# Low parts of the down chunks by VectorE instead of an adding DMA, and other rates for the conditioning products

## The chip, the cores and the metric

One Trainium2 chip, and one of its cores. The metric is the device time of one execution of the whole program in microseconds (us). Engines are named as in the profile: PE is TensorE's matmul, PEld its weight load, DVE is VectorE, ACT is ScalarE, POOL is GpSimd, SP is SyncE, which here only issues DMAs. Each engine runs its own list of instructions strictly in order; a name with a q (SPq, POOLq) is an engine's sequencer.

## What is computed

Two transformer blocks in float32 on 256 tokens of width 1024. The first block (attention of three kinds, a gated merge, an FFN with a short convolution) comes first and is not touched. The second block has two layers on a latent stream and a context stream, each conditioned by products of a vector with a weight `w_mod`:

```python
m_lat = adaln_mod(c, w_mod[l], b_mod[l])          # 9 x 1024 numbers a layer, for each stream
m_ctx = adaln_mod(c_ctx, w_mod[l], b_mod[l])[None]
x_lat = ffn_sublayer(x_lat, m_lat, 0, norm_g[l, 0], ffn_w_in[l, 0], ffn_w_out[l, 0])
x_ctx = ffn_sublayer(x_ctx, m_ctx, 0, norm_g[l, 0], ffn_w_in[l, 0], ffn_w_out[l, 0])
...   # the mixer: attention, Fourier branch, gates; then the second FFN of the layer

def swiglu(u, w_in, w_out):
    a, b = jnp.split(u @ w_in, 2, axis=-1)
    return (jax.nn.silu(a) * b) @ w_out

def ffn_sublayer(x, m, i, g, w_in, w_out):
    u = modulate(rms_norm(x, g), m, i)
    return x + 0.5 * m[:, 3 * i + 2][:, None] * swiglu(u, w_in, w_out)
```

In layer 1 the context stream ends after the mixer's keys and values, so the last FFN runs on the latent stream alone. An FFN has a hidden width of 2816, which is 22 pieces of 128.

## The kernel before

**Products in three.** Every float32 weight chunk of 128 partitions is split into a high part `wh`, rounded to the matmul's input type, and a low part `wl = wr - wh`; each product is three matmuls (lines 500 to 502): high by high, low by high, high by low. A chunk comes through three rings: `wr` (the raw weights, 3 buffers, loaded from SP's queue, line 434), `wh` and `wl` (5 buffers each). `prefetch` makes the split ahead of the matmuls, and `load_to` asks for the raw chunk three further on; that DMA waits in SP's queue until the raw buffer of three chunks before is free, and everything behind it on SP waits too.

**Two ways to the low part.** `split_high` makes `wh` on ACT (line 439). For weights whose name is in `ADDED` it also writes `-wh` into `wl` on ACT (line 444), and a DMA issued by POOL adds the raw chunk to it (line 445); the raw buffer is free when that DMA has landed. For all others `split_low` makes one subtraction on DVE (line 453), and the raw buffer is free after it:

```python
if self.order[i][0].tensor.name[3:].startswith(ADDED):       # split_high
    self.nc.scalar.activation(lo[:, :n], r[:, :n], AF.Copy, scale=-1.0)
    self.nc.gpsimd.dma_start(lo[:, :n], r[:, :n], accum_op=ALU.add)
self.nc.vector.tensor_tensor(lo[:, :n], r[:, :n], h[:, :n].bitcast(F32), op=ALU.subtract)   # split_low
```

**The FFNs of the second block.** In order: FFN (0,0); mixer 0; FFN (0,1); FFN (1,0); mixer 1; FFN (1,1). The two in the middle, (0,1) and (1,0), are the "seven" FFNs: most of their up products are taken in pairs of chunks with seven products in the place of eight (`ffn7`, matmuls on line 1451). The pairs' weights are prepared by `pair_prep` with sums on DVE (lines 362, 372, 381, 405). Their downs come in four groups of 5, 5, 6 and 6 hidden pieces; a group has 8 chunks (one for 128 outputs each) of 640 or 768 columns. The first two chunks of a group run together in both "mm" banks of PSUM, then one chunk after the other; each ends in two additions into `x` on DVE (line 1184), which free the bank for the chunk after the next. After three of the groups comes a stretch of pairs, and the first 6 hidden pieces of a seven FFN are made in the ordinary way.

**Conditioning products.** `w_mod` is 288 units of 128x512. A unit is one DMA into one of three `wm` buffers (line 633, on SP's queue between the weight loads) and one or two products with a row sum on DVE (line 647; two for both streams, one where only the latent stream is wanted): 512 products in all. They are spread as filler: after a chunk with a tick, `run` adds a rate to a credit and runs a unit for every whole one. The rates are constants: `MR[2]` for FFN (0,0), `MR[3]` and `MR[4]` for the heads of mixer 0 and 1, `MG` for the end of a mixer (from its Fourier part on: chunks `w_ao`, `w_fo`, `w_o`), `MD` for the downs of the seven FFNs and the projections that follow. `mod_cols` runs what is still missing when a column is needed.

Of the kernel before, what the change touches and what calls it, by code (L numbers as in the profile page):

```python
# [35 lines left out]
SCRATCH = 1024  # L36
NRAW = 3
NMOD = 3
MR = (1.2, 0.5, 1.9, 0.0, 0.0)
MG = 2.0  # L40
MD = 1.3
ADDED = ("ffn_up01", "ffn_up10", "ffn_down01", "ffn_down10")
AT0 = (2.25, 0.5, 3.25, 5.5, 8, 2.25, 4, 2.67, 0.1)
AT1 = (2, 0.5, 3, 5, 9, 2, 4.5, 4, 0.1)
GL1 = (0, 1, 1, 1, 1, 1, 1, 1)
# [205 lines left out]
class Net:  # L251
# [185 lines left out]
    def split_high(self, i, n):  # L437
        h = self.wp.tile([P, D], F32R, name="wh")
        self.nc.scalar.activation(h[:, :n], self.raws[i][:, :n], AF.Copy)  # L439
        self.wts[i] = (h,)  # L440
        if self.order[i][0].tensor.name[3:].startswith(ADDED):

# [241 lines left out]
    def b1_attention(self):  # L684
# [288 lines left out]
        ev += [(4, lambda: nx["n"].ssq(self.sxx))] + [(ME[0] + ME[1] * d, norm_u, d) for d in range(KD)]  # L973
        ev += [(ME[2], mem_load), (ME[2] + 1, table2, 1), (22, self.setup_late), (31, mods_on, MR[0]), (60, mods_on, MR[1]), (AB[3] + 1, table3, 1)]
        ev += [(ME[3] + ME[4] * d, me, "sqadd", d) for d in range(KD)] + [(ME[5], me, "ssq"), (ME[6], mem_rb)]
# [118 lines left out]
    def b1_ffn(self):  # L1094
# [60 lines left out]
        def u(d):  # L1155
            n["y"].u(d, self.c00[:, 1, 1], self.c00[:, 0, 1])
# [7 lines left out]
        def rest():  # L1164
            self.cur = self.c00
            self.mod_rate = MR[2]
            self.pending = [(0.5 * d, lambda d=d: u(d)) for d in range(PC[0], KD, 2)]
# [219 lines left out]
    def ffn7(self, wu, groups, gh, gl, up, down):  # L1387
# [67 lines left out]
        def front(f, i):  # L1455
            self.pair_prep(i, 2)
            s = st[f] = {"w": self.prep[i], "c": self.bank("ps")[:, CTX], "e": self.bank("ps")[:, CTX]}
            product(1, s["w"], "ab", 0, s["c"], True)
            nc.scalar.activation(s["e"], s["c"], AF.Copy)
# [130 lines left out]
        for g, (f0, f1) in enumerate(groups):  # L1590
# [6 lines left out]
            if g:  # L1597
                self.do(drain, prev[-1], prev[-2])
            self.do(self.set_rate, MD)
            down(g)  # L1600
            if f < NF:
                self.steps.insert(len(self.steps) - 1, ((), lambda f=f: front(f, self.pairs[0]), (), False))
        self.do(self.set_rate, MD)

# [32 lines left out]
    def mixer(self, l, both, nxt):  # L1637
# [53 lines left out]
        self.do(heads)  # L1691
        self.do(self.set_rate, MR[3 + l])
        bg = []
# [17 lines left out]
        def gates(d, at="mm"):  # L1711
            return [x for j in range(2) for x in self.chunk(w[28 + j * KD + d], cs, gate_done(d, j), at,
                                                           pieces=4 if both else 2)]
# [133 lines left out]
        for t in range(2):  # L1847
            self.do(f_split, nt // 2 - 1, t)
        self.do(f_const)
        self.do(self.set_rate, MG)  # L1850
        rest = [x for d in range(ng, 2 if both else KD) for x in gates(d, "ps")]
        if not both:
            self.steps += rest[:OO]
# [264 lines left out]
```

## Time and profile before

| | us |
|---|---|
| median of three runs | 2565.48 (2562.25 to 2566.53) |
| the profiled execution | 2564.71 |
| its span | 2562.9 |
| PE busy | 2468.2 (96%) |
| DVE busy | 1811.1 (71%) |
| ACT busy | 1230.7 (48%) |
| POOL busy | 136.0 (5%) |

The stages of the second block in the profiled execution: FFN (0,0) from 503 to 853 us, mixer 0 to 1278, FFN (0,1) to 1672, FFN (1,0) to 2056, mixer 1 to 2346, the last FFN to the end. A row of the order of time has its start, its duration, engine, line, operation and tiles; brackets at its end give how long the engine had stood idle and what released it. Matmuls overlap, so the time from one start to the next is shorter than the duration of one.

### The profile page before, as it was taken

The numbers are of one execution on the slowest core, as the hardware profiler recorded it, in microseconds if no ns is written. First come the engines' busy times: TensorE is split into PE (matmuls) and PEld (weight loads), VectorE is DVE, ScalarE is ACT, GpSimd is POOL, SyncE is SP. The second block draws the span as 40 slices with busy tenths as digits, with TensorE's granted clock in tenths as the row PEclk, the third lists the DMA queues.
The fourth block names the chain that finished last, engine by engine and source line by source line (L and its number), as shares of the span: only waits on it lengthen the run. The fifth ranks groups of instructions, "written<-read, shape, count | busy, mean of one in ns | idle before, by whom it ended". The sixth has DMA issues, their size and how long they took to land. (4 is left out here: it accounts for less than half of the span.)

```text
span 2562.9 us, 41264 instructions
## 1 busy us (share of the span) xinstructions
PE 2468.2 (96%) x15912; PEld 2214.6 (86%) x15912; DVE 1811.1 (71%) x3659; ACT 1230.7 (48%) x2175; POOL 136.0 (5%) x152
## 2 busy tenths in 40 slices
PE   8999999999999999999999899999999999998998
PEld 6899899998888878888887898888898878888998
DVE  6878787767878768688747577546577557777765
ACT  6755566542222356532354454554454545654543
POOL 0000200200000000100011100111100100000000
PEclk9999999999999999999999999999999999999999
DMA  7666456555655421155666536576536533355654
GB/s 252 211 216 224 138 183 195 160 165 170 204 189 182 136 75 58 56 168 185 193 154 177 137 103 189 146 168 178 128 118 185 145 120 105 112 178 190 190 186 132
DMA packets 144918, 410.16 MB, mean 160 GB/s; under 512 B 16273, under 2 KB 23121, under 8 KB 144337
## 3 DMA queue, kind: packets, MB, share of 16 engines
q1 hardware_dynamic: 132048, 371.87, 44.7%
q0 software_dynamic: 12672, 35.66, 8.0%
q8 instruction: 125, 2.05, 0.3%
q14 instruction: 73, 0.59, 0.1%
HBM read 370.73 MB, written 4.23 MB: 146 GB/s over the span
## 5 line engine op out<-in xcount | busy, mean ns | idle before, releaser
L439 ACT ACTIVATE wh<-wr 128x1024 fp32r<-128x1024 f32 (+2 forms) x503 | 506.5, 1009 | 425.1 <-DMA wr<-in_ffn_down 82.8
L453 DVE TENSOR_TENSOR wl<-wr,wh 128x1024 fp32r<-128x1024 f32 (+1 forms) x415 | 497.0, 1203 | 42.3 <-ACT wh L439 42.0
L501 PE MATMUL ps<-uh,wl 128*128 128x256 f32 (+2 forms) x1432 | 453.4, 317 | 4.6 <-DMA wl<-wr 2.7
L502 PE MATMUL ps<-ul,wh 128*128 128x256 f32 (+2 forms) x1432 | 453.4, 317 | 3.3 <-DVE ul L151 1.9
L500 PE MATMUL ps<-uh,wh 128*128 128x256 f32 (+2 forms) x1432 | 454.3, 317 | 0.1
L647 DVE SCALAR_TENSOR_TENSOR mjunk<-wm,cvec 128x512 bf16<-128x512 f32 x512 | 327.4, 686 | 67.0 <-DMA wm<-in_w_mod 66.6
L500 PE MATMUL mm<-gh,wh 128*128 128x512 f32 (+1 forms) x860 | 299.4, 348 | 32.6 <-DVE x L1184 26.3
L501 PE MATMUL mm<-gh,wl 128*128 128x512 f32 (+1 forms) x860 | 297.6, 346 | 0.8 <-DMA wl<-wr 0.8
L502 PE MATMUL mm<-gl,wh 128*128 128x512 f32 (+1 forms) x860 | 297.2, 346 | 0.0
L501 PEld LDWEIGHTS ps<-uh,wl 128*128 128x128 f32 x1432 | 273.6, 191 | 24.0 <-DMA wl<-wr 3.4
L502 PEld LDWEIGHTS ps<-ul,wh 128*128 128x128 f32 x1432 | 273.2, 191 | 22.1 <-DVE ul L148 2.3
L500 PEld LDWEIGHTS ps<-uh,wh 128*128 128x128 f32 x1432 | 273.1, 191 | 18.1 <-ACT uh L144 0.3
L500 PE MATMUL mm<-uh,wh 128*128 128x256 f32 (+1 forms) x840 | 281.7, 335 | 0.8 <-ACT uh L142 0.7
L502 PE MATMUL mm<-ul,wh 128*128 128x256 f32 (+1 forms) x840 | 271.6, 323 | 0.5 <-DVE ul L153 0.5
L501 PE MATMUL mm<-uh,wl 128*128 128x256 f32 (+1 forms) x840 | 271.1, 323 | 0.0
L500 PEld LDWEIGHTS mm<-gh,wh 128*128 128x128 f32 x860 | 165.3, 192 | 59.1 <-issue 15.0
L502 PEld LDWEIGHTS mm<-gl,wh 128*128 128x128 f32 x860 | 165.2, 192 | 20.5
L501 PEld LDWEIGHTS mm<-gh,wl 128*128 128x128 f32 x860 | 165.3, 192 | 20.3 <-DMA wl<-wr 1.2
L500 PEld LDWEIGHTS mm<-uh,wh 128*128 128x128 f32 x840 | 158.8, 189 | 25.1 <-issue 9.2
L502 PEld LDWEIGHTS mm<-ul,wh 128*128 128x128 f32 x840 | 158.5, 189 | 14.3 <-DVE ul L153 0.9
L501 PEld LDWEIGHTS mm<-uh,wl 128*128 128x128 f32 x840 | 158.9, 189 | 11.6
L1184 DVE SCALAR_TENSOR_TENSOR x<-mm,mc,x 128x256 f32<-128x256 f32 x212 | 93.4, 478 | 84.5 <-PE mm L502 84.4
(431 smaller groups left out, 5011.3 us busy)
## 6 DMA issues: line engine op xcount, KB each, us to landing
wr<-in_ffn_up SPq DMA_DIRECT2D x186, 512.0 KB, 4.2
wm<-in_w_mod SPq DMA_DIRECT2D x288, 256.0 KB, 4.0
wr<-in_w_in SPq DMA_DIRECT2D x106, 512.0 KB, 3.7
wr<-in_w_ffn_up SPq DMA_DIRECT2D x44, 512.0 KB, 4.2
wr<-in_ffn_down SPq DMA_DIRECT2D x48, 384.0 KB, 3.4
wr<-in_ffn_down SPq DMA_DIRECT2D x32, 512.0 KB, 3.7
wr<-in_w_v SPq DMA_DIRECT2D x24, 512.0 KB, 3.6
wl<-wr POOLq DMA_DIRECT2D x24, 512.0 KB, 5.9
```

Of the source, the lines that this page charges most:

```text
L439: self.nc.scalar.activation(h[:, :n], self.raws[i][:, :n], AF.Copy)
L453: self.nc.vector.tensor_tensor(lo[:, :n], r[:, :n], h[:, :n].bitcast(F32), op=ALU.subtract)
L500: mm(ps, lhsT=h, rhs=xh[k][:, cs], start=start and i == 0, stop=False)
L501: mm(ps, lhsT=lo, rhs=xh[k][:, cs], start=False, stop=False)
L502: mm(ps, lhsT=h, rhs=xl[k][:, cs], start=False, stop=stop and i == len(kk) - 1)
L647: nc.vector.scalar_tensor_tensor(junk, w, 1.0, self.cvec[:, v, cs], op0=ALU.mult, op1=ALU.mult, accum_out=self.m[l][:, v, h, j:j + 1])
L1184: self.nc.vector.scalar_tensor_tensor(x, ps[:, off:off + S], c[:, 2, v, d:d + 1], x, op0=ALU.mult, op1=ALU.add)
```

## The change

```diff
-MR = (1.2, 0.5, 1.9, 0.0, 0.0)
-MG = 2.0
-MD = 1.3
-ADDED = ("ffn_up01", "ffn_up10", "ffn_down01", "ffn_down10")
+MR = (1.2, 0.5, 2.3, 0.0, 0.4)
+MG = (2.3, 0.8)
+MD = 1.0
+ADDED = ("ffn_up01", "ffn_up10")
...
-        self.do(self.set_rate, MG)
+        self.do(self.set_rate, MG[l])
```

Two things change. The 64 down chunks of the seven FFNs get their low part from DVE (line 453); the 64 copies on ACT (line 444) and the 64 adding DMAs on POOL (line 445) go. And the 512 conditioning products stand elsewhere. Counted in the lists of instructions, before and after: 70 and 70 ahead of FFN (0,0), 194 and 234 in it, 138 and 152 in mixer 0, 48 and 19 in FFN (0,1), 24 and 19 in FFN (1,0), 38 and 18 in mixer 1. Of the 18 left in mixer 1, 6 stand in its value projections and 12 among its heads; before, 7 stood there, none among the heads, and 31 in its end. No matmul is added, removed or moved.

DVE's list in the second group of downs of FFN (0,1), before (`x<-mm,mc,x` are the additions that free a bank, `mjunk` the conditioning products):

```order
L1184 SCALAR_TENSOR_TENSOR x<-mm,mc,x 128x256 x4
L647 SCALAR_TENSOR_TENSOR mjunk,m_116<-wm,cvec 128x512 x4
L1184 SCALAR_TENSOR_TENSOR x<-mm,mc,x 128x256 x2
L647 SCALAR_TENSOR_TENSOR mjunk,m_116<-wm,cvec 128x512 x2
L1184 SCALAR_TENSOR_TENSOR x<-mm,mc,x 128x256 x2
L647 SCALAR_TENSOR_TENSOR mjunk,m_116<-wm,cvec 128x512 x4
L381 TENSOR_TENSOR wl<-wr,wh 128x1024
L1184 SCALAR_TENSOR_TENSOR x<-mm,mc,x 128x256 x2
```

The same place after:

```order
L453 TENSOR_TENSOR wl<-wr,wh 128x640 x2
L1184 SCALAR_TENSOR_TENSOR x<-mm,mc,x 128x256 x4
L647 SCALAR_TENSOR_TENSOR mjunk,m_116<-wm,cvec 128x512 x2
L453 TENSOR_TENSOR wl<-wr,wh 128x640 x2
L1184 SCALAR_TENSOR_TENSOR x<-mm,mc,x 128x256 x2
L647 SCALAR_TENSOR_TENSOR mjunk,m_116<-wm,cvec 128x512
L453 TENSOR_TENSOR wl<-wr,wh 128x640
L1184 SCALAR_TENSOR_TENSOR x<-mm,mc,x 128x256 x2
```

Low parts of 640 columns now stand between the additions, and a chunk is followed by one or two products where it was two or four.

DVE's list in the end of mixer 1, from one `w_fo` chunk to the next, before (`th` are the gated sums that free a bank, `mh` and `ml` the merged sum's parts):

```order
L1786 SCALAR_TENSOR_TENSOR ml_23835<-th_22701,mh_23827 128x256
L647 SCALAR_TENSOR_TENSOR mjunk,m_116<-wm,cvec 128x512 x2
L453 TENSOR_TENSOR wl<-wr,wh 128x1024
L1775 SCALAR_TENSOR_TENSOR th_23167<-th_23167,mm 128x256
L647 SCALAR_TENSOR_TENSOR mjunk,m_116<-wm,cvec 128x512 x2
L453 TENSOR_TENSOR wl<-wr,wh 128x1024
L1775 SCALAR_TENSOR_TENSOR th_23400<-th_23400,mm 128x256
L647 SCALAR_TENSOR_TENSOR mjunk,m_116<-wm,cvec 128x512 x2
L453 TENSOR_TENSOR wl<-wr,wh 128x1024
L1783 SCALAR_TENSOR_TENSOR th_22983<-th_22983,mm 128x256
```

The same place after:

```order
L1786 SCALAR_TENSOR_TENSOR ml_23867<-th_22737,mh_23859 128x256
L453 TENSOR_TENSOR wl<-wr,wh 128x1024
L1775 SCALAR_TENSOR_TENSOR th_23215<-th_23215,mm 128x256
L453 TENSOR_TENSOR wl<-wr,wh 128x1024
L1775 SCALAR_TENSOR_TENSOR th_23454<-th_23454,mm 128x256
L453 TENSOR_TENSOR wl<-wr,wh 128x1024
L1783 SCALAR_TENSOR_TENSOR th_23027<-th_23027,mm 128x256
```

No product is left there; the rest stands as it stood.

DVE's list in the first group of downs of FFN (0,0), from its second chunk's additions on, before:

```order
L1184 SCALAR_TENSOR_TENSOR x<-mm,mc,x 128x256 x2
L647 SCALAR_TENSOR_TENSOR mjunk,m_115<-wm,cvec 128x512 x4
L453 TENSOR_TENSOR wl<-wr,wh 128x768
L1184 SCALAR_TENSOR_TENSOR x<-mm,mc,x 128x256 x2
L647 SCALAR_TENSOR_TENSOR mjunk,m_115<-wm,cvec 128x512 x4
```

The same place after:

```order
L1184 SCALAR_TENSOR_TENSOR x<-mm,mc,x 128x256 x2
L647 SCALAR_TENSOR_TENSOR mjunk,m_115<-wm,cvec 128x512 x6
L453 TENSOR_TENSOR wl<-wr,wh 128x768
L1184 SCALAR_TENSOR_TENSOR x<-mm,mc,x 128x256 x2
L647 SCALAR_TENSOR_TENSOR mjunk,m_115<-wm,cvec 128x512 x4
```

About every third tick there now has three units, that is six products, where each had two; 24 ticks of FFN (0,0) and mixer 0 are of that kind.

## Rows read from the trace of the kernel before

**Rows 1.** Busy time by stretch; first column start and end, second its length.

```profile
core 0: us, PE busy (x) PEld busy (x) DVE busy (x) ACT busy (x) POOL busy (x), PEclk, DMA share, GB/s
642.20:676.60 34.40, 34.40 (x266) 33.28 (x266) 32.79 (x90) 8.16 (x9) 0.00 (x0) 1.00 0.63 204
...
1085.00:1270.00 185.00, 185.00 (x832) 151.49 (x831) 149.38 (x344) 59.97 (x80) 0.69 (x1) 1.00 0.55 176
1397.00:1444.50 47.50, 46.25 (x387) 45.84 (x386) 33.96 (x52) 25.41 (x45) 1.72 (x2) 1.00 0.30 83
1444.60:1479.60 35.00, 27.81 (x107) 21.55 (x106) 19.75 (x47) 12.15 (x18) 5.23 (x6) 0.90 0.75 205
2090.00:2270.00 180.00, 178.94 (x1157) 154.32 (x1156) 126.76 (x272) 101.53 (x213) 5.79 (x7) 1.00 0.37 116
2280.00:2342.00 62.00, 47.50 (x336) 45.47 (x335) 50.64 (x114) 18.16 (x28) 0.00 (x0) 0.87 0.66 218
2360.00:2540.00 180.00, 179.70 (x1495) 179.50 (x1495) 121.84 (x224) 85.55 (x119) 0.70 (x1) 1.00 0.57 179
```

**Rows 2.** PE's waits, 1360 to 2056 us: total us, times, longest.

```profile
PE mm L500 <- DVE x L1184: 26.3, 15, 6.0
PE mm L500 <- ACT sq L93: 4.9, 2, 4.4
```

**Rows 3.** The chain that ended last, around 1473 us.

```profile
1460.08 3.68 DMA wl<-wr
...
1463.81 0.33 SPq L434
...
1464.19 5.68 DMA wm<-in_w_mod
...
1472.33 0.88 DVE x L1184 x2
```

**Rows 4.** PE and DVE in order of time, first downs of FFN (0,1).

```profile
1368.67 1.66 DVE L1184 SCALAR_TENSOR_TENSOR x<-mm,mc,x 128x256 f32<-128x256 f32 x4
...
1369.69 0.47 PE L500 MATMUL mm<-gh,wh 128*128 128x512 f32 x1 [3.29 <-DVE x L1184]
```

**Rows 5.** At the lower clock, 1400 to 2060 us: first of five stretches, sum.

```profile
1472.50:1479.30 6.80, 5.95 (x14) 4.73 (x15) 6.73 (x14) 1.77 (x2) 0.00 (x0) 0.50 0.64 227
...
sum 27.20, PE 21.74 PEld 19.13 DVE 19.66 ACT 8.26 POOL 3.50; mean PE 4.35 PEld 3.83 DVE 3.93 ACT 1.65 POOL 0.70
```

**Rows 6.** DMA issues: out and in, queue, count, KB each, median us to landing.

```profile
wm<-in_w_mod SPq DMA_DIRECT2D x288, 256.0 KB, 4.0
...
wl<-wr POOLq DMA_DIRECT2D x32, 384.0 KB, 4.7
```

**Rows 7.** Groups of DVE instructions by form: count, busy us, mean ns of one.

```profile
L647 DVE SCALAR_TENSOR_TENSOR mjunk<-wm,cvec 128x512 bf16<-128x512 f32 x512 | 327.4, 686 | 67.0 <-DMA wm<-in_w_mod 66.6
...
L453 DVE TENSOR_TENSOR wl<-wr,wh 128x768 fp32r<-128x768 f32 x24 | 22.8, 952 | 2.8 <-ACT wh L439 2.7
```

**Rows 8.** DVE in order of time, last pairs of FFN (0,1)'s first stretch.

```profile
1430.90 0.42 DVE L1498 TENSOR_TENSOR u<-tp,u 128x256 f32<-128x256 f32 x1 [2.05 <-ACT u L1494]
...
1437.63 0.42 DVE L1503 TENSOR_TENSOR u<-tp,u 128x256 f32<-128x256 f32 x1 [5.71 <-PE tp L1451]
```

**Rows 9.** PE's waits, 2280 to 2342 us: total us, times, longest.

```profile
PE mm L500 <- DVE th L1783: 5.5, 3, 2.4
PE mm L500 <- DVE th L1775: 4.0, 3, 2.1
PE mm L500 <- DVE x L1184: 3.8, 1, 3.8
```

**Rows 10.** Stretches at the lower clock between 2290 and 2347 us, summed.

```profile
sum 20.30, PE 16.40 PEld 15.84 DVE 15.54 ACT 8.21 POOL 0.00; mean PE 5.47 PEld 5.28 DVE 5.18 ACT 2.74 POOL 0.00
```

**Rows 11.** DVE in order of time, first downs of FFN (0,0).

```profile
667.78 0.69 DVE L647 SCALAR_TENSOR_TENSOR mjunk<-wm,cvec 128x512 bf16<-128x512 f32 x1 [0.46 <-DMA wm<-in_w_mod]
...
670.15 0.87 DVE L1184 SCALAR_TENSOR_TENSOR x<-mm,mc,x 128x256 f32<-128x256 f32 x2
```

## The prediction

> **What bounds the kernel now.** I read the table of busy time first: PE is busy 96% of the span and no other engine over 71%, so the program can only become shorter where PE stands still or runs slowly. The views were then read in this order: busy time by stretch, PE's waits, the chain of waits, the order of time, the granted clock.
>
> By stretch [rows 1] there are two kinds of stage. In the first downs of FFN (0,0), the end of mixer 0, the heads of mixer 1 and the last FFN, PE is busy practically all the time, whatever DVE does beside it. In a down stretch of a seven FFN it is busy 27.8 of 35.0 us, with DVE at 19.8 and ACT at 12.2: nobody is full there, so somebody waits in a circle. In the end of mixer 1 PE has 47.5 of 62.0 us, and DVE, at 50.6, is the fullest engine.
>
> The waits name who ends them. From 1360 to 2056 us PE waits 26.3 us for the additions that free a bank (L1184), and 4.9 us for a square on ACT that follows such an addition [rows 2]. The additions are late for a reason far from DVE. The chain before the longest wait, 6.0 us, runs backwards like this [rows 3]: the additions at 1472.33 stand on DVE behind conditioning products; these wait for a `wm` load that takes 5.68 us; SP issued it only at 1464.19, since ahead of it in SP's list stood a weight load that could go at 1463.81 and no sooner; and that one waited for its raw buffer, which an adding DMA held from 1460.08 on. So one slow low part stops SP, SP stops the conditioning products, these stop the additions, and these stop PE.
>
> The waits cost a second time. In five stretches of 1400 to 2060 us the granted clock stands at 0.50, the lower of the two levels (1.2 instead of 2.4 GHz), each time right behind or inside a wait of PE of two us or more; PE is busy 21.7 us in them [rows 5]. In three such stretches around the end of mixer 1 it is busy 16.4 us [rows 10]. Half of such time is lost.
>
> **The low parts of the downs.** Removed are 64 adding DMAs of 4 to 5 us each [rows 6] and 64 copies on ACT. Added are 64 subtractions on DVE, of which one of 768 columns took 0.95 us [rows 7]; one of 640 I put at 0.8 by the ratio of columns, so 32 x 0.95 + 32 x 0.8 = 56 us of DVE. A raw buffer is then free about 1 us after its high part instead of 5. What is gained: of the 31.2 us in rows 2, the two waits of 3.3 us at the very first downs of the two seven FFNs stay. They have another cause: the additions stand behind DVE's sums for the pairs [rows 4]. Some four waits of 0.4 us stay too, where both banks are in use at the start of a group. The rest is 31.2 - 6.6 - 1.6 = 23 us, and I take 23, with 12 as the lower bound (half of the additions late for DVE's own work) and 28 as the upper (smaller waits that the two rows don't hold). Of the lost clock, 21.7 / 2 = 10.9 us, I take 9.5, bounds 5 and 11.
>
> What it costs: five chunks' low parts of a group of eight stand among its additions, and the first ones beside the pairs. In the group of 1444 to 1480 us DVE has 15 us to spare in 35 [rows 1], and it loses products there as well (19 instead of 48 in the whole FFN). A chunk has 5 x 3 matmuls and takes PE 3.5 us (27.8 us less 3.0 lost to the clock, over 107 matmuls, times 15, rows 1 and 5); DVE's work for it is 0.8 (low part) + 0.9 (two additions) + 0.7 (one product) = 2.4 us. The low parts beside the pairs come in the last two pairs, where DVE stood idle for 2.1 and 5.7 us waiting for PE and ACT [rows 8]; each fits into one such gap. One doesn't: in the first downs a low part stands right between DVE's sums and the four additions that PE waits for [rows 4], so that wait grows from 3.3 to about 4.1 us, twice: 1.6 us. Bounds 0 and 6 (one us in each of six groups). If the cover is gone, the whole 56 us is the price; that is a rival below.
>
> **Products out of the end of mixer 1.** 31 products go from there. Each takes DVE up to 0.69 us [rows 7], together about 20 of the 50.6 us that DVE is busy, and with them the times when DVE waited for `wm`. Next in line is then PE itself: it has 47.5 us of work, some of it at the lower clock. The last FFN is the nearest row for a stage with chunks of the same size and no products: PE 179.7 of 180.0 us [rows 1]. The waits shown sum to 5.5 + 4.0 + 3.8 = 13.3 us, all of them for DVE [rows 9]. I take 11.5 (bounds 7 and 14), since the merged sum still passes from DVE to ACT and back; and of the clock, 16.4 / 2 = 8.2 us, 7.5 (bounds 3 and 8).
>
> **Products into other stages.** FFN (0,0) gets 40 more, 40 x 0.69 = 28 us of DVE's time in a stage where PE has not waited. In its first downs DVE is at 32.8 of 34.4 us [rows 1]. There a chunk takes 34.4 / 8 = 4.3 us, and with three units instead of two DVE needs up to 0.95 + 0.9 + 6 x 0.69 = 6.0. The sixth chunk ends at 642.2 + 6 x 4.3 = 668.0 and its additions began at 670.15 [rows 11], 2.1 us late; they may end 4.3 us late before the eighth chunk waits. Two bursts ahead of it add 4 x 0.69 = 2.8: 2.1 + 2.8 + 0.9 = 5.8, a wait of 1.5, and with a later `wm` (0.46 us once before, rows 11) I take 2 us, bounds 0 and 8; a stretch at the lower clock behind it may cost 1.7 more, and I count it. The end of mixer 0 gets 14 more in 185 us, where DVE is at 149 [rows 1]: 0.5, bounds 0 and 3. The heads of mixer 1 get 12 single ones, 8 us beside 53 us of idle DVE [rows 1]; they stand between steps of a softmax on which PE later waits, but chunks lie between: 1.2, bounds 0 and 6. SP's list has as many loads as before; in the first FFN a weight load now stands behind up to three `wm` loads, but weights there are split four chunks ahead.
>
> **The sum.** Gains 23 + 9.5 + 11.5 + 7.5 = 51.5; costs 1.6 + 2 + 1.7 + 0.5 + 1.2 = 7.0. The profiled execution took 2564.7, 1.8 more than its span and 0.8 less than the median of the runs. 2564.7 - 44.5 + 0.8 = **2521 us**. All bounds at their best give 61 of gain and no cost, 2504; all at their worst 27 of gain and 25 of cost, 2563.
>
> **Rivals.** (a) The circle is broken, but the downs are then late for something else, their loads or DVE's order, and half of the 32.5 us of the seven FFNs stays: 2537. For it: in these stretches the DMA engines' share is 0.75 [rows 1]. Against: the adding DMAs, as many bytes as the loads of the same chunks, were part of it.
> (b) DVE takes the place of the DMA: all of the 32.5 us stays in a new wait, and only mixer 1 gains: 2553. For it: the additions do stand behind the low parts in DVE's list. Against: 2.4 us of work in 3.5.
> (c) Slower: the bursts of three units in FFN (0,0) and mixer 0. There are three `wm` buffers, so after a burst the next load can only be issued when its first unit is done, and it takes 4.0 us to land [rows 6]. If DVE waits for what is left after that unit's two products, 4.0 - 2 x 0.69 = 2.6 us, at each of the 24 bursts, and PE with it, that is 62 us in place of the 3.7 counted: 2579. It decides where DVE has less than these 2.6 us to spare in a chunk. Against: most chunks there are 24 matmuls of 512 columns, where one of the first downs is 30 of 256 and 3 of 512, so 4.3 x 24 / 18 = 5.7 us, in which the load lands before the next unit; only the short first downs lie near it.
> (d) Slower: all low parts on the path, since DVE is the scarce engine beside the pairs (34.0 of 47.5 us, rows 1): 2521 + 56 = 2577. The Trainium skill, "Perfetto Trace Analysis", section "Optimizing Scalar/DVE Operations", holds that where DVE is saturated some of its work had better go to another engine; by that rule this change goes the wrong way, and the trace agrees for the start of the pairs alone, not for the downs.
>
> **How the numbers follow.** The forecast, near 2521, has 0.72; (a) 0.13, (b) 0.06, (c) 0.04, (d) 0.03, and 0.02 is left for no change. The range of 8 in 10 takes in (a) and most of the bounds and leaves out (b), (c), (d): 2504 to 2546. About 0.2%, 5 us, is what a measurement can tell from no change. Faster by more holds the forecast, (a) and most of (b): 0.90; within 0.2% 0.04; slower 0.06.
>
> **What would show it.** In the profile after: no adding DMA of 320 or 384 KB; PE's waits for L1184 from 1360 us to the end of FFN (1,0) about 10 us instead of 26; two waits of some 4 us at the first downs; no wait of over 2 us in the other downs, and the granted clock full there. The end of mixer 1 takes about 42 us instead of 62, with PE the fullest engine. FFN (0,0) stays within 4 us of its 350. Wrong would be: waits of PE for L1184 or `wl` in the downs with DVE busy throughout; a string of waits for `wm` in FFN (0,0); or gaps that go while the time does not.

## The result, and the profile after

The changed kernel takes 2507.93 us (median, 2505.86 to 2511.65) where the kernel before takes 2564.07 beside it; the ratio is 0.978, with a 95% interval of 0.9765 to 0.9799. The forecast was 2521 (2504 to 2546): the time lies in the range, and the gain is 56 us where 44.5 were expected.

Busy time of each engine after, with its share of the span:

```profile
span 2504.0 us, 41140 instructions
PE 2447.6 (98%) x15912; PEld 2197.3 (88%) x15912; DVE 1861.9 (74%) x3723; ACT 1190.6 (48%) x2111; POOL 80.3 (3%) x88
```

DVE does 51 us more than before, PE is busy 21 us less, and the span is 59 us shorter. The same matmuls as in [rows 1], by stretch (columns as there; PE issues the same matmuls in the same order in both kernels, so each stretch was cut at the same matmul):

```profile
638.70:676.10 37.40, 34.82 (x266) 33.02 (x265) 34.56 (x94) 8.16 (x9) 0.00 (x0) 1.00 0.64 202
1084.60:1275.60 191.00, 187.61 (x831) 152.40 (x830) 156.06 (x366) 60.51 (x80) 0.72 (x1) 0.99 0.57 183
1402.90:1448.70 45.80, 45.80 (x386) 45.80 (x386) 33.19 (x49) 23.50 (x43) 0.00 (x0) 1.00 0.23 71
1448.80:1473.80 25.00, 24.64 (x107) 19.73 (x106) 19.90 (x40) 8.60 (x12) 0.00 (x0) 1.00 0.59 198
2050.70:2232.60 181.90, 180.00 (x1157) 154.23 (x1156) 133.62 (x294) 101.24 (x213) 5.78 (x7) 1.00 0.40 129
2242.70:2283.40 40.70, 40.31 (x336) 39.92 (x335) 31.59 (x58) 18.38 (x28) 0.00 (x0) 1.00 0.51 159
2299.50:2480.80 181.30, 181.00 (x1495) 180.79 (x1494) 121.63 (x223) 86.27 (x119) 0.70 (x1) 1.00 0.58 178
```

The second group of downs (107 matmuls) takes 25.0 us where it took 35.0, with PE busy to 24.6 of it. The end of mixer 1 takes 40.7 instead of 62.0. The first two rows are longer: 3.0 us in the first downs of FFN (0,0), 6.0 in the end of mixer 0.

The main waits of PE after (total us, times, longest), in four groups: the two seven FFNs, the end of mixer 1, FFN (0,0), and the end of mixer 0.

```profile
PE mm L500 <- DVE x L1184: 9.1, 5, 4.0
PE ps L501 <- DMA wl<-wr: 2.7, 2, 1.4
...
PE mm L500 <- DVE th L1775: 0.4, 1, 0.4
...
PE mm L500 <- DVE x L1184: 2.6, 2, 1.9
...
PE mm L500 <- ACT mh L1785: 2.3, 2, 1.5
PE ps L1826 <- DVE z L493: 1.1, 1, 1.1
```

Against [rows 2], 26.3 us have become 9.1 and the wait for a square is gone; against [rows 9], 13.3 us have become 0.4.

To see where the 59 us came from, I subtracted the starts of each matmul and the next in the two traces, matmul by matmul, and sorted the differences: time in which PE had no matmul (idle), matmuls in a stretch at the lower clock in one of the two traces (clock), and the rest. In us, + is gained:

| stage | sum | idle | clock | rest |
|---|---|---|---|---|
| first block (not touched) | 3.8 | 0.6 | 3.1 | 0.2 |
| FFN (0,0) | -4.0 | -2.6 | 0.0 | -1.3 |
| mixer 0 | -5.5 | -3.0 | -1.5 | -1.1 |
| FFNs (0,1) and (1,0) | 44.2 | 29.7 | 10.1 | 4.4 |
| value projections and heads of mixer 1 | -1.2 | -0.4 | 0.0 | -0.8 |
| end of mixer 1 | 23.0 | 14.1 | 7.8 | 1.2 |
| last FFN | -1.2 | 0.0 | 0.1 | -1.4 |

The 3.8 us of the first block are a difference between executions (in the twelve other runs below it lies between -0.7 and 4.0), so a single row is good to a few us where it is small. The rest of 4.4 us in the two FFNs fits what a wait costs beyond itself: across a wait the step from one start to the next is 0.1 to 0.2 us longer than the usual step and the idle time together (in the trace after, 4.39 us from 1371.88 to 1376.27, of which 3.99 are idle and 0.23 is the usual step).

### The profile page after: what moved, and what is told of

Its sections match the earlier page's. It is cut to its first block, busy times and chain, and to the rows that moved or that the text cites. A ratio compares the mean times of both kernels' runs of the same rounds, so it can differ in the third digit from the quotient of the medians.

```text
span 2504.0 us, 41140 instructions
## 1 busy us (share of the span) xinstructions
PE 2447.6 (98%) x15912; PEld 2197.3 (88%) x15912; DVE 1861.9 (74%) x3723; ACT 1190.6 (48%) x2111; POOL 80.3 (3%) x88
## 3 DMA queue, kind: packets, MB, share of 16 engines
q8 instruction: 125, 2.05, 0.3%
HBM read 370.73 MB, written 4.23 MB: 150 GB/s over the span
## 4 chain that ended last, share of the span: by engine, by line
PE 74%; DVE 11%; DMA 7%; issue 4%; ACT 4%; SPq 0%; POOL 0%; DVEq 0%; POOLq 0%; ACTq 0%
PE mm L500 10%; PE mm L502 10%; PE mm L501 10%; PE ps L1451 9%; PE ps L502 8%; PE ps L501 8%; PE ps L500 7%; DVE wl L453 3%; DMA wm<-in_w_mod 3%; DVE mjunk L647 2%; PE op L1451 2%; PE tp L1451 2%; DMA wr<-in_w_ffn_up 1%; PE ps L1907 1%; ACT wh L439 1%
## 5 line engine op out<-in xcount | busy, mean ns | idle before, releaser
L453 DVE TENSOR_TENSOR wl<-wr,wh 128x1024 fp32r<-128x1024 f32 (+2 forms) x479 | 553.6, 1163 | 40.3 <-ACT wh L439 39.5
L501 PEld LDWEIGHTS mm<-uh,wl 128*128 128x128 f32 x840 | 159.2, 190 | 11.6
L1184 DVE SCALAR_TENSOR_TENSOR x<-mm,mc,x 128x256 f32<-128x256 f32 x212 | 93.4, 478 | 78.7 <-PE mm L502 77.9
```

The costliest lines, as they stand in the source:

```text
L501: mm(ps, lhsT=lo, rhs=xh[k][:, cs], start=False, stop=False)
L1184: self.nc.vector.scalar_tensor_tensor(x, ps[:, off:off + S], c[:, 2, v, d:d + 1], x, op0=ALU.mult, op1=ALU.add)
```

## Experiments

Each kernel was timed in rounds beside the kernel before, which took 2562.2 to 2564.1 us. In the table stands the gain on it by stage, from the same matmul by matmul comparison of one profiled execution each ("sevens" are FFNs (0,1) and (1,0)); first block, heads and last FFN are left out, none of their entries is over 4.0 us either way. The profiled executions of traffic_only and hold_raw took 8 and 5 us more than their medians, so their entries are a little on the slow side.

| kernel | median | ratio, 95% interval | FFN (0,0) | mixer 0 | sevens | end of mixer 1 |
|---|---|---|---|---|---|---|
| the change | 2507.9 | 0.9765 to 0.9799 | -4.0 | -5.5 | 44.2 | 23.0 |
| low_only | 2522.7 | 0.9830 to 0.9859 | 0.0 | 0.2 | 40.0 | -0.7 |
| rates_only | 2545.8 | 0.9922 to 0.9951 | -5.7 | -6.4 | 8.1 | 22.7 |
| wm_pool | 2577.2 | 1.0042 to 1.0072 | -1.8 | 0.3 | -12.1 | -2.2 |
| low_dma | 2544.3 | 0.9911 to 0.9945 | -6.3 | -5.4 | 10.3 | 23.1 |
| traffic_only | 2518.4 | 0.9810 to 0.9857 | -5.6 | -6.2 | 25.6 | 22.9 |
| hold_raw | 2570.7 | 1.0019 to 1.0046 | -5.5 | -7.5 | -21.5 | 22.6 |
| sums_early | 2494.7 | 0.9724 to 0.9754 | -6.8 | -5.5 | 55.7 | 22.9 |
| old_filler | 2513.4 | 0.9797 to 0.9826 | -1.1 | 0.8 | 40.3 | 11.1 |
| even_filler | 2501.3 | 0.9738 to 0.9774 | 0.4 | 0.4 | 39.5 | 21.6 |
| no_adds | 2496.1 | 0.9722 to 0.9753 | -1.4 | 0.6 | 44.9 | 23.3 |
| both_steps | 2490.3 | 0.9702 to 0.9734 | -3.8 | -4.8 | 58.7 | 22.9 |
| two_units | 2490.1 | 0.9698 to 0.9732 | -0.2 | 0.6 | 54.8 | 21.2 |

**One half of the change each.** low_only is the kernel before with

```diff
-ADDED = ("ffn_up01", "ffn_up10", "ffn_down01", "ffn_down10")
+ADDED = ("ffn_up01", "ffn_up10")
```

> The kernel before with one part of the change alone: the 64 down chunks' low parts by DVE, all rates of the conditioning products as before (so 48 and 24 products stay in the seven FFNs and 31 in the end of mixer 1). Theory: the raw buffer that an adding DMA held was what stopped SP, the products and the additions; then PE's waits for L1184 from 1360 to 2056 us fall from 26 us to about 10 although the products stay, the lower clock goes from the downs, and the gain is about 35 us: 2529 (2522 to 2540), with the end of mixer 1 and FFN (0,0) as before. Rival: the number of products among the downs was what made the additions late; then DVE, with 56 us more to do and no product less, gains 10 us at most: 2554 or more.

rates_only is the changed kernel with `ADDED` as before.

> The changed kernel with the other part alone: all rates as in the change, the down chunks' low parts by the adding DMA as before. Theory: the circle stays in the downs, with fewer wm loads to be stopped in it, so at least 15 of the 26 us of waits for L1184 stay; the end of mixer 1 gains 23, FFN (0,0), mixer 0 and the heads of mixer 1 lose 10, the downs gain about 10: 2541 (2533 to 2552). Rival: fewer products among the downs suffice, and the low parts were harmless; then the waits go here too and it takes 2517 or less.

Measured: 2522.7 and 2545.8. The two halves gain 40 and 17 us, together the 56 of the change. PE's longest group of waits in the sevens, in low_only:

```profile
PE mm L500 <- DVE x L1184: 9.5, 6, 4.0
```

and in rates_only:

```profile
PE mm L500 <- DVE x L1184: 24.1, 10, 5.1
```

With 72 products left in the sevens the waits go (9.5 us); with 38 and the adding DMAs they stay (24.1). So the low parts broke the circle, and the number of products did not make it. Products are what the end of mixer 1 hangs on: it gains 22.7 us in rates_only, where only their places changed.

**Is it the raw buffer, or the bytes?** An adding DMA both holds a raw buffer and loads the DMA engines. low_dma was meant to bring back the bytes alone, in the changed kernel's `split_low`:

```diff
+            self.nc.gpsimd.dma_start(self.idle[:, :n], h[:, :n].bitcast(F32), accum_op=ALU.add)
```

> The changed kernel, and beside each of the 64 subtractions of the downs a DMA on POOL's queue that adds as many bytes, read from wh, to a buffer in memory that nobody reads. It loads the DMA engines as the removed transfers did, but holds no raw buffer. Theory (the held buffer): within 5 us of the change, 2505 to 2513, no wait of over 2 us in the downs but the two at the first ones. Rival (the transfers took the loads' share of the DMA engines): the loads are late again and half or more of the 43 us that the two FFNs gained is lost: 2530 to 2550.

Measured: 2544.3, the rival's time, but not in the rival's way. The waits for L1184 in the sevens are 9.5 us, as with the change; new ones stand in the pairs and at the norms (PE's waits; lines past the edits have slightly higher numbers in this and the next two kernels):

```profile
PE ps L1455 <- ACT u L1498: 10.4, 4, 4.3
...
PE tp L124 <- POOL rstd L118: 6.1, 2, 3.9
```

POOL in order of time, one of the added DMAs:

```profile
1471.29 0.86 POOL L455 DMA_DIRECT2D idle<-wh  x1 [6.16 <-DMA idle<-wh]
```

All these DMAs write one buffer, so each waits in POOL's list for the one before; POOL's step of the norm stands behind them, and `wh`, their source, is held far past its use (ACT waits 11.6 us in six places for such a DMA before it can write the next pair's `wh`). The experiment had made a new held buffer, and says nothing on the bytes. The next two mend that: eight buffers in turn, a tiny copy that sets the time, and two kernels that differ in the source alone. (The buffers lie in DRAM, where the adding DMAs of before wrote SBUF: 27.30 MB are written to HBM in both kernels, 4.23 in the one before. So the route is alike in the two, but it is not the old one.)

```diff
+            self.nc.gpsimd.tensor_copy(self.st.tile([P, 1], F32, name="tick", bufs=1), h[:, :1].bitcast(F32))
+            self.nc.gpsimd.dma_start(self.dd.tile([P, 768], F32, name="idle")[:, :n], SRC, accum_op=ALU.add)
```

traffic_only has `self.cvec[:, 0, :n]` for SRC, hold_raw `r[:, :n]`.

> The changed kernel, and beside each of the 64 subtractions of the downs a DMA on POOL's queue that adds as many bytes to a buffer in memory that nobody reads. Its source is the constant cvec, so it holds neither a raw buffer nor a wh, and eight such buffers in turn keep POOL from waiting for the DMA before; a tiny copy of one column of wh on POOL sets its time. Theory (the held raw buffer made the waits): within 6 us of the change, 2505 to 2514. Rival (the bytes on the DMA engines made the loads late): 2525 or more, with waits in the downs or at the first pairs behind them.

> The same with one difference: the source of the added DMA is the chunk's raw buffer, which is so held until that DMA has landed, as before the change; the low part itself still comes from DVE. Theory (the held raw buffer): SP stops again, the weights of the next pairs and the wm loads are late, the additions behind them too: waits of PE of 2 to 6 us near the ends of the groups, 2530 to 2550. Rival (the bytes alone): the same time as with the constant as source, within 5 us.

Measured: 2518.4 (2512.7 to 2526.7) and 2570.7 (2563.2 to 2580.2); both are above the ranges of the theory, the second by 21 us. The bytes cost some 10 us; holding the raw buffer with the same bytes costs 52 more, and the kernel is then slower than before. The added DMAs of 384 KB took 7.7 us to land in the one and 6.1 in the other (medians), so the second has no slower transfers. The 52 us are not what the held buffer cost in the kernel before: hold_raw has DVE's subtractions as well, and its DMAs, into DRAM, hold the buffer longer than the adding ones did (6.1 us against 4.7, [rows 6]). It also has no copies on ACT (line 444), so the waits do not need them; what these 64 copies cost by themselves was not measured. PE's waits in the sevens for the additions (L1187 is the line of L1184 in these two), in traffic_only:

```profile
PE mm L503 <- DVE x L1187: 15.0, 7, 4.0
```

and in hold_raw:

```profile
PE mm L503 <- DVE x L1187: 39.9, 13, 8.3
```

The chain before hold_raw's wait of 8.3 us (start, duration, what):

```profile
1473.34 4.64 DMA idle<-wr
...
1478.03 0.33 SPq L434
...
1478.41 0.47 SPq L636
...
1478.93 8.75 DMA wr<-in_ffn_up
...
1488.83 0.88 DVE x L1187 x2
```

It reads as [rows 3] did: the raw buffer is held, SP's weight load goes only when it is free (1478.03), another weight load two places behind it takes 8.75 us, and the additions come late. One link differs: DVE waits not for `wm` but, for 10.08 us, for the first weight of the next pair, which is the load issued at 1478.03.

```profile
1486.96 1.23 DVE L381 TENSOR_TENSOR wl<-wr,wh 128x1024 fp32r<-128x1024 f32 x1 [10.08 <-ACT wh L377]
```

**Is `wm` the link?** The prediction let the chain run over the `wm` load. wm_pool is the kernel before with these loads on another queue:

```diff
-            self.nc.sync.dma_start(t, self.a["w_mod"][72 * l + j, h])
+            self.nc.gpsimd.dma_start(t, self.a["w_mod"][72 * l + j, h])
```

> The kernel before with one edit: the wm loads are issued from POOL's queue in place of SP's, so that a weight load that waits for its raw buffer no longer stands ahead of them. The adding DMAs and all rates stay. Theory (SP's list passes the held buffer on to the products): the products come in time, PE's waits for L1184 in the downs fall from 26 to about 12 us and the time by some 20 us, 2535 to 2555; what stays is weights that are late themselves. Rival (the lateness is DVE's own work, or the DMA engines'): no change, within 5 us of 2564. A POOL that stands at a wm load's wait would hold the adding DMAs behind it; if so, new waits for wl appear in the ups and downs and the time rises.

Measured: 2577.2, slower by 15 us than the kernel before beside it (2562.5). PE's waits for the additions in the sevens, 26.3 us before, are now:

```profile
PE mm L500 <- DVE x L1184: 36.5, 15, 6.0
```

DVE's idle time from 1400 to 2010 us by what ended it, in the kernel before:

```profile
DVE mjunk L647 <- DMA wm<-in_w_mod: 42.1, 10, 8.6
...
DVE wl L381 <- ACT wh L377: 11.6, 2, 6.8
```

in wm_pool:

```profile
DVE mjunk L647 <- DMA wm<-in_w_mod: 31.6, 12, 6.3
...
DVE wl L381 <- ACT wh L377: 19.1, 4, 8.3
```

and in rates_only:

```profile
DVE wl L381 <- ACT wh L377: 31.0, 4, 8.7
...
DVE mjunk L647 <- DMA wm<-in_w_mod: 11.5, 5, 4.0
```

L381 makes the first low part of the next pair's weight, and it stands on DVE ahead of the last chunk's additions. Its raw load is one of those that SP keeps back. With fewer products (rates_only) or with `wm` elsewhere (wm_pool), that wait takes over. So neither the theory (some 20 us faster) nor the rival (no change) held: SP has two ways to the additions, the products and the pair's weight, and closing one leaves the other. The third case in the expectation, that POOL's queue holds things up, is there in part: PE's waits for `wl` from the adding DMAs rise only from 2.4 to 3.7 us, but DVE once waits 8.1 us for such a DMA, and a `wm` load now stands behind an adding DMA that waits for ACT. How much of the loss is the queue's was not measured.

**The first downs.** In the changed kernel the two longest waits left are the two predicted ones, of 4.0 us. DVE and PE in order of time at the first:

```profile
1372.24 1.23 DVE L1406 TENSOR_TENSOR bl<-l,bh 128x1024 fp32r<-128x1024 f32 x1 [1.13 <-ACT bh L1405]
1373.38 1.22 DVE L1439 TENSOR_TENSOR ul<-h,uh 128x1024 fp32r<-128x1024 f32 x1
1374.52 0.82 DVE L453 TENSOR_TENSOR wl<-wr,wh 128x640 fp32r<-128x640 f32 x1
1375.26 1.65 DVE L1184 SCALAR_TENSOR_TENSOR x<-mm,mc,x 128x256 f32<-128x256 f32 x4
...
1376.27 0.47 PE L500 MATMUL mm<-gh,wh 128*128 128x512 f32 x1 [3.99 <-DVE x L1184]
```

sums_early makes each of the four sums one up pair sooner:

```diff
-        up(2)
-        for f, step in zip(range(3, F7), (sum_a, sum_e, sum_t)):
+        for f, step in zip(range(2, F7), (sum_a, sum_e, sum_t, sum_b)):
             self.do(step)
             up(f)
-        self.do(sum_b)
         self.do(place_a)
```

> The changed kernel with one edit: in the two seven FFNs the four sums for the pairs are each made one up chunk pair earlier, so that the last of them no longer stands between the last up and the first four additions on DVE. Theory (these sums make the two 4.0 us waits at the first downs): the waits fall below 1 us each, the two stretches at the lower clock behind them (3.4 and 6.8 us) go as well, 2 x 3.3 + 10.2 / 2 = 11.7 us less: 2496 (2493 to 2502). Rival (the low part and the split of the last sum's sources, or the hidden pieces, are as late without it): at least 3 us of each wait stay, 2504 or more.

Measured: 2494.7, ratio 0.974. The wait at the same matmul, and DVE's additions, which now wait for PE (sums_early, in order of time):

```profile
1373.88 1.66 DVE L1184 SCALAR_TENSOR_TENSOR x<-mm,mc,x 128x256 f32<-128x256 f32 x4 [1.93 <-PE mm L502]
...
1374.90 0.48 PE L500 MATMUL mm<-gh,wh 128*128 128x512 f32 x1 [0.36 <-DVE x L1184]
```

The granted clock is full throughout the sevens there. Of the 13.3 us, 11.5 stand in the sevens: 7.3 of idle time, in the two waits, and the rest the lower clock behind them. The time lies in the theory's range.

**Where should the products stand?** old_filler is the changed kernel with the rates 1.9, 2.0 and 1.3 of before outside mixer 1.

> The changed kernel with the rates of FFN (0,0), mixer 0's end and the downs as before (1.9, 2.0, 1.3); the rates of mixer 1 stay as in the change. So 40 and 14 products go back from the first two stages, 34 of them into the downs and 20 into mixer 1, whose end gets some. Theory: the 3.6 us of FFN (0,0) and the 5.5 of mixer 0 came from bursts of three units and return; the downs lose 3, mixer 1's end 8 to 12 for about 14 products: 2510 (2504 to 2517). Rival (DVE is full in the downs now, so each of the 34 products costs its 0.69 us there): 2525 or more.

Measured: 2513.4. FFN (0,0) and mixer 0 are back to within 1.1 us of before, and the sevens pay 3.9 us for 34 more products. Mixer 1's end loses 12 us for 16, but most of that in one place, since the last seven stand in a row in front of the last FFN's first column, and PE waits 6.7 us there. That wait, and DVE in order of time, two of the seven with what they waited for:

```profile
PE mm L500 <- DVE x L1184: 6.7, 1, 6.7
...
2281.64 0.69 DVE L647 SCALAR_TENSOR_TENSOR mjunk<-wm,cvec 128x512 bf16<-128x512 f32 x1 [1.44 <-DMA wm<-in_w_mod]
...
2285.31 0.69 DVE L647 SCALAR_TENSOR_TENSOR mjunk<-wm,cvec 128x512 bf16<-128x512 f32 x1 [1.51 <-DMA wm<-in_w_mod]
```

even_filler is sums_early with MR[2] = 1.9, MG[0] = 2.0, MD = 1.7; no_adds is even_filler with `ADDED = ()`.

> The kernel with the early sums, and the rates 1.9 in FFN (0,0), 2.0 in mixer 0's end and 1.7 in the downs in place of 2.3, 2.3 and 1.0: no bursts of three units in the first two stages, 88 products in the downs of the seven FFNs where there were 38, none in the end of mixer 1. Theory (bursts cost, single products beside free time of DVE do not): FFN (0,0) and mixer 0 give back 3.6 and 5.5 us, the downs lose 6 (they lost 4 with 72 products): 2491 (2487 to 2497) against 2494.7. Rival (the downs' DVE is the next bound): the downs lose 15 or more, 2500 and up.

> The same, and the low parts of the 24 ordinary up chunks of the seven FFNs by DVE too, so that no adding DMA is left. Theory (what held for the downs holds there: a raw buffer that is free early, and 24 x 1.22 us beside DVE's free time): the two waits of 1.3 us for wl in the ups go, and a part of the waits around the norms: 3 us less than with the adding DMAs (1 to 6). Rival (in the ups DVE now has the early sums and the products to do as well): low parts stand behind sums of 1.2 us each, PE waits for wl, 5 us or more slower.

Measured: 2501.3 and 2496.1. even_filler is a miss; its time is the rival's. The first two stages gave back 13 us on sums_early, but the sevens lost 16 for 50 more products, 0.32 us each. Ten waits for the additions stand there, 9.1 us together, and at one of 1.95 us DVE's list reads (even_filler, in order of time):

```profile
1375.55 0.69 DVE L647 SCALAR_TENSOR_TENSOR mjunk<-wm,cvec 128x512 bf16<-128x512 f32 x1 [0.47 <-DMA wm<-in_w_mod]
...
1378.01 1.22 DVE L381 TENSOR_TENSOR wl<-wr,wh 128x1024 fp32r<-128x1024 f32 x1
1379.15 0.82 DVE L453 TENSOR_TENSOR wl<-wr,wh 128x640 fp32r<-128x640 f32 x1
1379.88 0.86 DVE L1184 SCALAR_TENSOR_TENSOR x<-mm,mc,x 128x256 f32<-128x256 f32 x2
```

Four products in a row, the pair's low part and a chunk's low part are 4.3 us from the first start to the additions, in a chunk of about 3.5. no_adds gains 5.2 us (3 expected, 1 to 6), all of it in the sevens.

both_steps is sums_early with `ADDED = ()`; two_units is both_steps with the rates 2.0, 2.0, 1.25 and 0.6 among mixer 1's heads.

> The changed kernel with its own rates (2.3, 2.3, 1.0), the early sums, and no adding DMA at all (the 24 ordinary up chunks' low parts by DVE too). Theory (the two steps add up: 13.3 us for the sums, 5.2 for the ups' low parts): 2490 (2486 to 2494). Rival (with fewer products in the downs the ups' adding DMAs no longer hold anything up, or the early sums and the ups' low parts meet on DVE): no better than with the early sums alone, 2493 or more.

> The same with rates of 2.0 in FFN (0,0) and mixer 0's end, 1.25 in the downs and 0.6 among mixer 1's heads: no bursts of three units anywhere, and about 70 products in the downs, 20 fewer than where they lost 16 us and 30 more than in the change. Theory (the loss in the downs grows faster than their number, since it begins where two units stand in a row): the first two stages give back 7 us, the downs lose 5, the heads 1: 2489 (2484 to 2495), no difference that counts to the run beside it. Rival (each product in the downs costs 16/50 = 0.32 us from the first on): they lose 10, and it is 4 us or more behind the run beside it.

Measured: 2490.3 and 2490.1, the fastest kernels of the study, 17.6 us below the change. The two steps add up. With 64 products in the sevens instead of 38 two_units loses 3.9 us there, 0.15 each, half the price that even_filler paid; the first two stages give back 9, and mixer 1 with its 16 products more loses 2. Most of what is left of the difference lies in the untouched first block, which took 3.4 us longer in two_units. By the times the two can't be told apart.

A product in the sevens so has no one price: it is 0.15 us for 26 more, 0.11 for 34 more (old_filler), and 0.32 for 50 more, or 0.28 where no adding DMA is left (no_adds against both_steps, 13.8 us). Rows of four products and more on DVE's list are most frequent in the dear ones as well: none in the changed kernel, five in two_units, seven in old_filler, eleven in even_filler. Whether the number or the rows set the price these runs don't separate.

## Why the prediction came out as it did

**The low parts of the downs: right in cause, too small by 13.** Predicted were 23 us of waits less 1.6, and 9.5 of clock, net 30.9; measured 44.2. Not all of that is the low parts': low_only gained 40.0 in these stages, and the other 4.2 came with the fewer products, for which the sum had no term. The clock term holds (10.1), though its count does not: six stretches between 1400 and 2060 us stand at the lower clock, not five; the sixth, 1755.8 to 1762.6, is behind a wait of 3.3 us that was to stay. The waits that should stay hold as well: two of 3.99 and 4.02 us where 4.1 was said, 9.1 in all where "about 10" was said. One chunk's subtraction took 0.82 us at 640 columns (0.8 estimated) and 0.95 at 768. What was mis-sized is the sum over waits. I had added up the two rows of [rows 2]; the smaller ones, before the norms and in the pairs, went as well (that they hung on the same SP list is likely, but was not shown). Idle time fell by 29.7, which is even above the upper bound of 28. And a wait was priced at its idle time alone, where the 4.4 us of the rest come on top.

**How the held buffer reaches the additions: half right.** That the held buffer makes these waits is shown by hold_raw against traffic_only; what it was worth to take the adding DMAs out of the kernel before, buffer and bytes together, is the 40.0 us of low_only. The chain over `wm` was one of two; the other runs over the next pair's weight. It made no difference to the sum, since the change freed both, but anyone who had acted on the chain alone would have moved the `wm` loads and lost 15 us.

**The end of mixer 1: right.** Predicted 11.5 and 7.5; measured 14.1 idle and 7.8 clock, in 40.7 us where "about 42" was said. The idle term reached its upper bound because nothing was left in the place of the waits: for the merged sum's path over ACT, for which I had held back 1.8, PE does not wait at all, and the one wait left, 0.4 us, is for a gated sum (L1775).

**FFN (0,0): right in place; that the size was met is luck.** 2 and 1.7 of clock were predicted, 4.0 measured: 2.6 of idle time, no stretch at the lower clock, and 1.3 of rest, for which the sum had no term. Six other kernels with the same rates here (rates_only, low_dma, traffic_only, hold_raw, sums_early, both_steps) lost 3.8 to 6.8 us; in sums_early the lower clock did come, for 3.4 us behind a wait of 2.8. In the changed kernel PE waits twice, 0.65 and 1.93 us. DVE ahead of the second, which is at the eighth chunk as drawn, with a wait for `wm`:

```profile
666.88 0.69 DVE L647 SCALAR_TENSOR_TENSOR mjunk<-wm,cvec 128x512 bf16<-128x512 f32 x1
668.18 0.69 DVE L647 SCALAR_TENSOR_TENSOR mjunk<-wm,cvec 128x512 bf16<-128x512 f32 x1 [0.60 <-DMA wm<-in_w_mod]
...
669.41 1.22 DVE L453 TENSOR_TENSOR wl<-wr,wh 128x1024 fp32r<-128x1024 f32 x1
670.54 0.87 DVE L1184 SCALAR_TENSOR_TENSOR x<-mm,mc,x 128x256 f32<-128x256 f32 x2
```

**The end of mixer 0: the step that failed.** Predicted 0.5 with a bound of 3, measured 5.5 (4.8 to 7.5 in the same six kernels). The step averaged: 14 products in 185 us, in which DVE is busy 149. But they stand in bursts, and two bursts fell where PE waits for DVE soon after: ahead of the Fourier part's `z` (1.1 us), and ahead of the last two merged sums (0.83 and 1.48, with 3.4 us at the lower clock behind them):

```profile
1239.75 0.69 DVE L647 SCALAR_TENSOR_TENSOR mjunk<-wm,cvec 128x512 bf16<-128x512 f32 x1 [1.42 <-DMA wm<-in_w_mod]
...
1242.12 0.68 DVE L1775 SCALAR_TENSOR_TENSOR th<-th,mm 128x512 f32<-128x512 f32 x1
1242.72 0.68 DVE L647 SCALAR_TENSOR_TENSOR mjunk<-wm,cvec 128x512 bf16<-128x512 f32 x1
...
1245.16 1.22 DVE L453 TENSOR_TENSOR wl<-wr,wh 128x1024 fp32r<-128x1024 f32 x1
1246.30 0.68 DVE L1783 SCALAR_TENSOR_TENSOR th<-th,ps 128x512 f32<-128x512 f32 x1
```

The 1.42 us before the third unit is the mechanism of rival (c) at one of its 24 places; most of the others never reached PE, which has five such waits in the two stages. old_filler and two_units, without these bursts, lose nothing there.

**Heads of mixer 1: right in being small.** 1.2 predicted, 1.2 measured, of which 0.4 is idle time; that the two figures agree says little at this size.

**The rivals.** (a), (b) and (d) are out: half or all of the 32.5 us would have stayed, or 56 us been added, where 44.2 went. The Trainium skill, "Perfetto Trace Analysis", section "Optimizing Scalar/DVE Operations", which stood behind (d) with its advice for a saturated DVE, did not decide here: DVE took on 51 us more, from 71% to 74% of the span, and the downs became shorter. Its condition, a saturated DVE, holds only around the first downs, and there the price was the 0.7 us by which each wait grew. In even_filler the condition is met at another place, where DVE's list of 4.3 us does not fit into a chunk of 3.5; that moving work off DVE would help there was not tried.

In sum the errors were +13 in the sevens, +4 in mixer 1's end, -5 in mixer 0 and -1.2 in the last FFN; 3.8 us of the profiled difference lie in the untouched first block.

## What to carry to other kernels

A step that takes little of any engine's time is still dear if it holds a buffer for which an in-order queue waits: price the time of the buffer and what stands behind it in the queue, not the engine alone. When a wait's chain is followed back, look for the second way by which the same cause arrives before cutting a link. Filler work is to be costed where it stands, burst by burst, against the next thing that the main engine waits for: an average over a stage missed 5 us here. Nor has it one price: a product more in the sevens cost 0.11 to 0.15 us with up to 72 of them there, and about 0.3 with 88.

## What the runs showed of the hardware that was not expected

- The bytes were not free: with DMAs of 7.7 us into DRAM beside them (traffic_only), one 512 KB weight load took 11.13 us from 1467.02 on, where their median is 4.2 in the changed kernel, and DVE waited 5.10 us for the low part of the weight that was asked for just before it. The sevens took 18.6 us more than in the change in that execution, which was the slowest of its runs.
- A wait costs more than its length in two ways. In the sevens, 29.7 us of idle time went together with 10.1 at the lower clock and 4.4 of wider spacing. But not each wait is followed by the lower clock: behind the two waits of 4.0 us in the changed kernel it stood for 3.4 and 6.8 us, behind waits of 1.95 and 2.05 us in even_filler not at all.
- The clock also differs between executions of the same code: the untouched first block had 3.1 us less of its cost in the profile after than in that before.
